# Tap loads ahead of a restacking, 4 KB reads of block inputs, and two kinds of stores on GpSimd's queue, in a hybrid encoder block

## The chip, the cores and the metric

The kernel runs on one core of a Trainium2 chip. A core has a matrix engine (PE), a vector engine (DVE), a scalar engine (ACT), GpSimd (POOL) and SyncE (SP), which here does nothing but issue DMAs. Each engine works off its own instructions in program order; an instruction that waits holds up all that stand behind it on its engine. DMAs are issued by SP, ACT or POOL and carried by 16 DMA engines. The metric is the device time of one execution in microseconds; it is compared as the median of several runs.

## The reference, cut to what matters

One encoder layer for a sequence of 1024 tokens of width 1024, in float32. Every result below is computed; the norms' small helpers are left out.

```
h = RMSNorm_pre(x)
z, xbc, dt_raw, u = split(h @ W_in)            # 1024 | 1536 | 32 | 1024 columns
# SSD mixer (16 heads of 64, 2 groups, state 128, chunks of 128, both directions)
xbc = silu(depthwise_conv5(xbc) + conv_b)
xs, b, c = split(xbc);  dt = softplus(dt_raw + bias);  a = -exp(a_log)
y_f = ssd_scan(xs, dt[fwd], a[fwd], b, c);  y_b = the same on the flipped sequence
y_ssd = group_rms_norm((y_f + y_b + xs * d_skip) * silu(z)) * norm_w
# S5 mixer (64 groups of 16 channels, 64 complex states, both directions)
h_t = A_g h_{t-1} + B_g u_t;   y = Re(C_g h_t) of both directions + d_skip * u
g = gelu(y);   y_s5 = g * sigmoid(g @ glu_w + glu_b)
x = x + RMSNorm_post(concat(y_ssd, y_s5) @ W_out)
# feed-forward
h = RMSNorm_pre(x)
x = x + RMSNorm_post((silu(h @ w_gate) * (h @ w_up)) @ w_down)
```

## The kernel before, in words

A matmul with the precision of float32 is made of three with operands of fewer bits: each operand is split into a high and a low half (`hi`, `lo`), and high by high, low by high and high by low are summed (L276, L1170). All stages below hand tensors to each other over DRAM tiles whose names end in `_d`.

**Stages in order of time.** 0 to 100 us: norm of x, and tables of the S5 powers. 100 to 225: the columns u of the input projection in 8 blocks of 8 groups; `u_evac` (L570 and on) writes a block into `u_d` (8 stores, L580), and `load_u` (L519) reads it back with tokens and channels on partitions. From it come the chunk sums that the S5 recurrence runs over. Up to 420: the other 18 blocks of the projection (`blocks`, L1306: nine of xbc, dt, eight of z, called z0 to z7 here). Between them the S5 recurrence goes on, `pair_down` (L648) finishes it in eight pieces, each four DVE instructions (L651, L652), and *kernel batches* begin. Batch b covers four S5 groups: `xt_load` loads its constants, `c_open` and `c_dir` (L690 to L706) build powers `cp` on ACT and DVE, `k_mm` (L723) multiplies them on PE, and `k_out` (L729 to L731) copies the result to `lg`, adds to it on POOL and stores it into `k_d` from POOL's queue. The number `KC` says how many blocks before the end of the loop over `blocks` batch 0 is opened: at block n the batch n - 18 + KC is opened, and the one before it is multiplied. Four batches are done within the loop.

**The tap stage**, 420 to 520 us, yields the S5 outputs in 16 pieces. `y_mm(i)` (L812 to L814) needs on PE: the taps `W0(i)`, which `w0_load` (L737) loads as a band matrix out of `k_d` from POOL's queue, 424 KB each; the inputs `Uy`, 512 KB for two pieces, loaded by `u_load` (L782) on SP out of `u_d`; `cp`; and the restacked states `AH`, which `restack(i)` (L792 to L802) writes: two POOL memsets for the first two, and eight ACT copies. `restack(0)` stands before the loop's last two blocks, `restack(1)` behind the loop, since it reads the states that the last `pair_down` leaves (and takes its buffer). The stage's loop keeps `w0_load` three pieces ahead, `k_mm` four, `restack` two.

**Up to 690 us** the gated unit of S5 (`glu`) and then `out_s5` run on PE, the second the S5 half of the output projection; its sums go to `m_d`. **SSD units** 0 to 7 (two heads each) are interleaved with these and with `out_g0` by a list scheduler with priorities (the names in `hpri`), so the order on every engine here is the scheduler's. A unit: transposes, `Xw` (L975, one direction on POOL and one on DVE), states `Sn` (PE L988, DVE L999), masked scores `M` (L1034, L1035, one of them on POOL), gating `yg` (L1058, L1059, partly on POOL), `sq`, and the split of the result into the two halves of `hl` (ACT L1073, DVE L1074). The halves are stored into `ch_d` and `cl_d` (L1075, L1076, 512 KB each). `cat` tiles are loaded from there.

**out_g0** (L1186 to L1201), about 840 to 930 us, adds the half of the output projection that the first four units feed, 16 pieces of 128 by 512: load the sum so far, `m` (two buffers, L1195), from `m_d`; load `cat` (L1160); 12 matmuls; add on DVE (L1199); store `m` to `m_d` (L1200). **The last quarter of the projection** follows with the block's first residual (`ld`, `ld2`, `ld3`, `xl`: L1675, L1681, L1686, L1690), and from 1050 us the feed-forward part, which PE fills.

Which queue issues a store is in a table: `Q` maps 's' to SP, 'a' to ACT, 'g' to POOL. 'cq' is the entry of L1075 and L1076, 'mq' the one of L1200.

Of the kernel before, what the change touches and what calls it, by code (L numbers as in the profile page):

```python
# [18 lines left out]
def _ap(t, off, dims):  # L19
# [5 lines left out]
KN = {'s0': -800,  # L25
 'sA': 8,
 'sB': 50,
 'sG': -8,
 'sF': 20,
 'rec': 0,  # L30
 'cb': 8,
 'kb': -100,
 'w0': 0,
# [35 lines left out]
 'gsp': [],  # L69
 'rsd': (1, 4, 7),  # L70
 'hq': 's',
 'cq': 's',
 'mq': 's',
 'pd': ['ef00', 'm00', 'xw1', 'yz0'],
 'yo': 0,
 'up': 0,
# [12 lines left out]
 'us': 'sagagaga',  # L89
 'pc': [],  # L90
 'pk': [0, 1, 3, 4],
 'KC': 7,
 'r1': 6,
 'r3': 0,
 'gs': 'asssssss',
# [36 lines left out]
def hymba_block(ctx, tc, P, out, dbg=None, upto=99):  # L132
# [12 lines left out]
    def pri(n):  # L145
        def deco(f):
            def g(*a, **k):
                with hpri(n):
                    return f(*a, **k)
            return g  # L150
        return deco

    act, dve, pool, pe, sp = nc.scalar, nc.vector, nc.gpsimd, nc.tensor, nc.sync
    aq, gq = nc.scalar, nc.gpsimd
# [18 lines left out]
    def dram(shape, name):  # L173
        return tc.dram_tile(shape, F32, name=name)

    u_d = dram([64, 8, 16, 128], "u_d")
    y12_d = dram([2, 128, 2, 1024 + 16], "y12_d")
    x12_d = dram([2, 128, 1024], "x12_d")
    k_d = dram([32, 64 * 240], "k_d")
# [336 lines left out]
    @pri("lu")  # L516
    def load_u(b):
        U = sa.tile([128, 8, 128], F32, tag="U", name="U")
        sp.dma_start(U, u_d[8 * b:8 * b + 8].rearrange("g s h k -> (s h) g k"))  # L519
        return U  # L520

    def pw4(t, d, n0, nn, g0, ng):
# [45 lines left out]
    def u_half(b, hf):  # L568
        ps = pacc()
        gemm(b, hTh[hf], hTl[hf], HF[0], ps)  # L570
        u_evac(b, hf, ps)

    def u_evac(b, hf, ps):
        if hf == 0:
            ups[b] = io.tile([128, 8, 128], F32, tag="io", name="up")
        up = ups[b]
        act.copy(up[:, ::-1, 64 * hf:64 * hf + 64], ps.rearrange("p (k s) -> p s k", s=8))
        if hf == 1:
            for g in range(8):
                {'a': aq, 's': sp, 'g': gq}[KN['us'][g]].dma_start(u_d[8 * b + g].rearrange("s h k -> h s k"), up[16 * g:16 * g + 16, :, :])  # L580

    def u_block(b):
        ensure(b + 1)
# [51 lines left out]
    def pair_powers():  # L635

        t = rt.tile([128, 2, 2, 32], F32, tag="rm", name="rm")
        a2 = rt.tile([128, 2, 2, 32], F32, name="rcA2")
        b2 = rt.tile([128, 2, 2, 32], F32, name="rcB2")
        dve.tensor_tensor(t, rcB, rcB, op=MUL)  # L640
        dve.tensor_tensor(a2, rcA, rcA, op=MUL)
        dve.tensor_tensor(a2, a2, t, op=SUB)
        dve.scalar_tensor_tensor(b2, rcA, 2.0, rcB, op0=MUL, op1=MUL)
        rcs.extend((a2, b2))
# [16 lines left out]
    def pair_down(d, c):  # L661

        t = ck.tile([128, 63, 2, 8], F32, tag="cacc", name="dn")
        advance(d, 2 - d, 1 + d, 63, 8 * c, 8, t)

    def run_steps(n):
        for _ in range(n):
            j = next(steps, None)
            if j is not None:
                rec_step(j)  # L670
# [6 lines left out]
    def xt_load(b):  # L677
        if b in xts_:
            return
        g0 = 4 * b  # L680
        xt = xts_[b] = ck.tile([128, 2, 4, 16], F32, tag="xtc", name="xtc", bufs=2)
        (gq if b < KN["xtb"] else sp).dma_start(xt.rearrange("p y g h -> p y (g h)"), x12_d.rearrange("y p f -> p y f")[:, :, 16 * g0:16 * g0 + 64])
        yk = yks[b] = ck.tile([128, 2, 80], F32, tag="yk", name="yk", bufs=3)
        (gq if b < KN["xtb"] else sp).dma_start(yk, y12_d[0][:, :, 16 * g0:16 * g0 + 80])
# [7 lines left out]
    def c_open(b):  # L692
        xt = xts_[b]
        pl = (ck, 4) if b % 7 < 4 else (yp, 3)
        cp = cps[b] = pl[0].tile([128, 2, 4, 9, 16], F32, tag="cp", name="cp", bufs=pl[1])
        act.copy(_ap(cp, 0, [[576 + 128, 2], [144, 4], [1, 16]]), xt[:, 0].unsqueeze(1).to_broadcast([128, 2, 4, 16]))

    def c_dir(b, d):
        g0 = 4 * b
        e = pool if 2 * b + d in KN['pcd'] else dve  # L700
        xt, cp = xts_[b], cps[b]
        tm = ck.tile([128, 4, 8, 16], F32, tag="tmc", name="tmc")
        dst = _ap(cp, 16 if d == 0 else 576 + 112, [[144, 4], [16 if d == 0 else -16, 8], [1, 16]])
        e.tensor_tensor(dst, spread(xt[:, 0], 8), pw4(arR, d, 1, 8, g0, 4), op=MUL)
        e.tensor_tensor(tm, spread(xt[:, 1], 8), pw4(aiR, d, 1, 8, g0, 4), op=MUL)
        e.tensor_tensor(dst, dst, tm, op=ADD)  # L706
# [3 lines left out]
    @pri("kb")  # L710
    def k_batch(b):
        k_mm(b)
        k_out(b)
# [19 lines left out]
    @pri("w0")  # L733
    def w0_load(b):

        W0 = W0s[b] = wst.tile([128, 960], F32, tag=("whi", "wlo")[b % 2], name="W0")
        gq.dma_start(W0[:, 0:848], bass.AP(tensor=k_d.tensor, offset=k_d.offset + 960 * b,  # L737
                                           ap=[[16, 8], [64 * 240, 16], [1, 848]]))
# [39 lines left out]
    @pri("u")  # L778
    def u_load(B):
        pl = (yp, 1) if B % 3 == 1 else (wst, 2)  # L780
        U = Us_[B] = pl[0].tile([128, 8, 128], F32, tag="raw", name="Uy", bufs=pl[1])
        sp.dma_start(U, u_d[8 * B:8 * B + 8].rearrange("g s h k -> (s h) g k"))  # L782

    AHs = []

    @pri("rs")
    def restack(b):

        if b < 4:

            AH = (ck if b < 2 else yp).tile([128, 2, 4, 128], F32, name=f"AH{b}", tag=("xpad", "cacc", "AH0", "AH1")[b])
            pool.memset(AH[:, 0, :, 0:1], 0.0)  # L792
            pool.memset(AH[:, 1, :, 127:128], 0.0)
            AHs.append(AH)
        AH, p0 = AHs[b if b < 2 else 2 + b % 2], 2 * b
        for d in range(2):
            for j in range(2):
                for comp in range(2):
                    src = SH[64 * j:64 * j + 64, d, (0 if d == 0 else 1):(127 if d == 0 else 128), comp, p0:p0 + 2]
                    dst = AH[64 * comp:64 * comp + 64, d, :, (1 if d == 0 else 0):(128 if d == 0 else 127)]  # L800
                    dst = dst.rearrange("p (q j) k -> p q j k", j=2)[:, :, j, :].rearrange("p q k -> p k q")
                    (dve.tensor_copy if 1 < b and 4 * d + 2 * j + comp in KN["rsd"] else act.copy)(dst, src)  # L802
# [408 lines left out]
    with tc.manual_schedule(engines={mybir.EngineType.DVE, mybir.EngineType.Activation, mybir.EngineType.PE}):  # L1211
# [28 lines left out]
        gemm_quarter(1, 4)  # L1240
        scale(5)
        u_evac(0, 0, ps0)
        for c in (6, 7):
            norm(c)
# [34 lines left out]
    for b in range(3, 8):  # L1279
        s_batch(b - 3, load_u(b - 3))  # L1280
        if b > 3:
            pair_up(b - 4)
        u_block(b)
    cv = None
    for b in range(5, 8):
        s_batch(b, load_u(b))
        pair_up(b - 1)
        xbc_block(b - 5)
        if cv:
            conv_silu(*cv, one=True)  # L1290
        if b > 5:
            cv = conv_taps(XORD[b - 6], sa)
# [44 lines left out]
    KC = KN["KC"]  # L1337
    downs = [(d, c) for c in range(4) for d in range(2)]
    with tc.manual_schedule():
        next(cvs)  # L1340
        pair_powers()
        for n, blk in enumerate(blocks):
            blk()
            run_steps(KN["r1"])
            next(cvs, None)
            if n == 10:
                run_steps(64)
            if n > 10:
                for _ in range(1 if n < 15 else 2):
                    if downs:  # L1350
                        pair_down(*downs.pop(0))
            b = n - NB + KC
            if 0 <= b < 4:
                c_open(b)
                c_dir(b, 0)
                run_steps(KN["r3"])
                c_dir(b, 1)
            if 0 < b < 5:
                k_batch(b - 1)
            if 0 <= b + 1 < 6:  # L1360
                xt_load(b + 1)
            if n == NB - 3:
                next(cvs, None)
                restack(0)
        restack(1)
        w0_load(0)
        w0_load(1)
        u_load(0)
    rst.close()
    hst[0].close()  # L1370
    hst[1].close()
# [23 lines left out]
    with tc.manual_schedule():  # L1395
        c_open(4)
        c_dir(4, 0)
        c_dir(4, 1)
        w0_load(2)
        u_load(1)  # L1400
        u_load(2)
        qs, oth = [], others()
        for i in range(16):
# [90 lines left out]
    B = {n: hp2.tile([128, 2, 4, 512], F32R, name="B" + n) for n in ("11", "21", "22")}  # L1494
# [85 lines left out]
    bank, us, ts_ = {}, {}, {}  # L1580
# [178 lines left out]
    for l in range(8):  # L1759
        b = MX["step"] * l  # L1760
# [11 lines left out]
        for q in range(2):  # L1772
            at(b + MX["ev"] + 0.6 * q, turn_evac, l, q)
            if l < 4 or q:
                n = "12"[q] + "12"[l // 4]
# [44 lines left out]
    for i in range(14, len(prods)):  # L1820
        p, n, m = prods[i]
# [68 lines left out]
    us, ts_ = C21, C22  # L1890
# [117 lines left out]
```

## Time and profile before

| | |
|---|---|
| median of 3 runs | 1652.74 us (1648.15 to 1654.55) |
| profiled execution | 1652.82 us, span 1651.1 us, mean granted PE clock 0.976 |
| PE | 1532.9 us busy, 93% |
| DVE | 1240.3 us, 75% |
| ACT | 719.5 us, 44% |
| POOL | 372.1 us, 23% |
| DMA | 271.59 MB, mean 164 GB/s |
| chain that ended last | PE 64%, DVE 11%, DMA 11%, ACT 6%, issue 5% |

The span runs from the first to the last instruction on record; the execution's time is 1.72 us longer. POOL's busy time doesn't include the DMAs that it issues. A share for PE over the whole span mixes stages in which it has no gap with stages in which it waits, so the rows below are of single stretches.

### The profile page before, as it was taken

The page shows a single profiled execution, that of the slowest core. Times are in us where ns is not written, and L with a number is a line of the kernel's source. Part 1 is how long each engine was busy: PE and PEld are TensorE (multiplying, and loading weights), DVE is VectorE, ACT ScalarE, POOL GpSimd, SP SyncE. Part 2 cuts the span into 40 slices and gives each one's busy share as a digit, 9 for nine tenths or more (in the row PEclk, how much of TensorE's full clock was granted, in tenths as well). Part 3 has the DMA queues.
Part 4 walks back from the last instruction along what each step waited for, and adds up shares of the span by engine and source line. Part 5 has one row for each costly group of instructions (what it writes and reads, how often), then busy time and mean ns, then how long its engine had stood idle before and what let it go on. Part 6 is the DMA issues. An engine that isn't in the chain of part 4 may idle for free.

```text
span 1651.1 us, 22178 instructions
## 1 busy us (share of the span) xinstructions
PE 1532.9 (93%) x7980; PEld 1256.0 (76%) x7980; DVE 1240.3 (75%) x1997; ACT 719.5 (44%) x1207; POOL 372.1 (23%) x403
## 2 busy tenths in 40 slices
PE   7999999999786989999999787999999999999997
PEld 6777788778675767777778675788888888788886
DVE  6549898877783777876666578788888878669677
ACT  6345532223776454544343387232322333345452
POOL 2100000000221120122210140555555555200001
PEclk9999999999998899999999998999999999999999
DMA  5554444432898557877688883233222221493234
GB/s 182 140 149 108 132 148 153 134 99 93 206 216 206 176 183 255 280 234 228 193 255 259 265 269 105 96 118 111 104 102 96 96 103 58 178 351 108 96 115 179
DMA packets 250001, 271.59 MB, mean 164 GB/s; under 512 B 29387, under 2 KB 190659, under 8 KB 249891
## 3 DMA queue, kind: packets, MB, share of 16 engines
q1 hardware_dynamic: 224515, 215.96, 42.3%
q0 software_dynamic: 12896, 33.83, 6.6%
q10 hardware_dynamic: 12480, 20.39, 3.5%
q8 instruction: 63, 1.03, 0.3%
q14 instruction: 47, 0.39, 0.1%
HBM read 185.23 MB, written 84.84 MB: 164 GB/s over the span
## 4 chain that ended last, share of the span: by engine, by line
PE 64%; DVE 11%; DMA 11%; ACT 6%; issue 5%; POOL 1%; SPq 1%; ACTq 0%; DVEq 0%; POOLq 0%
PE acc L276 17%; PE acc L1589 13%; PE ptmp L1589 10%; PE ptmp L1895 6%; PE acc L1895 5%; PE acc L1170 4%; DMA m<-m_d 2%; DMA m_d<-m 1%; DMA W<-k_d 1%; PE ptmp L557 1%; PE ptmp L1054 1%; PE ptmp L988 1%; DVE cacc L755 1%; PE ptmp L723 1%; DMA cl_d<-ghl 1%
## 5 line engine op out<-in xcount | busy, mean ns | idle before, releaser
L1170 PE MATMUL acc<-ohi,cat 128*128 128x512 f32 x512 | 173.3, 403 | 14.6 <-DVE m L1199 6.9
L276 PE MATMUL acc<-hTh,whi 128*128 128x512 f32 (+1 forms) x456 | 179.4, 394 | 0.4 <-ACT hTh L333 0.4
L276 PE MATMUL acc<-hTl,whi 128*128 128x512 f32 (+1 forms) x456 | 178.3, 391 | 0.5 <-DVE hTl L336 0.5
L276 PE MATMUL acc<-hTh,wlo 128*128 128x512 f32 (+1 forms) x456 | 177.8, 391 | 0.0
L1572 DVE TENSOR_TENSOR wop<-rawp,wop 128x512 fp32r<-128x512 f32 x120 | 137.5, 1147 | 17.9 <-ACT wop L1571 16.7
L1589 PE MATMUL ptmp<-T,wop 128*128 128x512 f32 x528 | 127.6, 398 | 4.1 <-ACT T L1745 3.7
L1589 PE MATMUL acc<-T,wop 128*128 128x512 f32 x528 | 125.7, 393 | 1.9 <-DVE T L1748 1.8
L1170 PEld LDWEIGHTS acc<-ohi,cat 128*128 128x128 f32 x512 | 97.4, 191 | 38.9 <-DVE m L1199 9.4
L1895 PE MATMUL ptmp<-dop 128*128 128x512 f32 x528 | 123.5, 396 | 2.9 <-DVE dop L1877 2.9
L1589 PE MATMUL acc<-B,wop 128*128 128x512 f32 x528 | 124.3, 391 | 0.0
L1589 PEld LDWEIGHTS ptmp<-T,wop 128*128 128x128 f32 x528 | 100.9, 191 | 27.2 <-ACT T L1745 3.9
L1895 PEld LDWEIGHTS ptmp<-dop 128*128 128x128 f32 x528 | 101.1, 192 | 24.6 <-DVE dop L1877 3.2
L1589 PEld LDWEIGHTS acc<-T,wop 128*128 128x128 f32 x528 | 98.8, 188 | 25.2 <-DVE T L1748 3.6
L1589 PEld LDWEIGHTS acc<-B,wop 128*128 128x128 f32 x528 | 99.0, 188 | 21.5
L1604 ACT ACTIVATE cg<-cg 128x512 f32<-128x512 f32 x44 | 27.8, 633 | 182.9 <-DVE cg L1602 182.9
L1571 ACT CAST wop<-rawp 128x512 fp32r<-128x512 f32 x120 | 70.3, 615 | 76.7 <-POOL rawp L1546 51.2
L1170 PE MATMUL acc<-olo,cat 128*128 128x512 f32 x256 | 101.7, 397 | 0.3 <-DVE olo L1134 0.3
L276 PEld LDWEIGHTS acc<-hTh,whi 128*128 128x128 f32 x456 | 86.5, 190 | 19.5 <-issue 1.9
L276 PEld LDWEIGHTS acc<-hTl,whi 128*128 128x128 f32 x456 | 86.6, 190 | 17.9 <-DVE hTl L336 1.0
L276 PEld LDWEIGHTS acc<-hTh,wlo 128*128 128x128 f32 x456 | 86.7, 190 | 17.2 <-DVE wlo L267 0.2
L1876 ACT CAST dop<-da 128x512 fp32r<-128x512 f32 x77 | 48.0, 623 | 99.5 <-PE acc L1895 38.8
L1610 POOL TENSOR_TENSOR cg<-cg 128x512 f32<-128x512 f32 x44 | 61.8, 1404 | 130.8 <-DVE cg L1605 130.2
(367 smaller groups left out, 3340.8 us busy)
## 6 DMA issues: line engine op xcount, KB each, us to landing
ff_d<-cg POOLq DMA_DIRECT2D x77, 256.0 KB, 2.3
da<-ff_d SPq DMA_DIRECT2D x35, 512.0 KB
raw<-in_w_in_dram SPq DMA_DIRECT2D x28, 512.0 KB
cat<-ch_d SPq DMA_DIRECT2D x48, 256.0 KB
cat<-cl_d SPq DMA_DIRECT2D x48, 256.0 KB
wd<-in_w_down_dram SPq DMA_DIRECT2D x44, 256.0 KB
rawp<-in_w_gate_dram SPq DMA_DIRECT2D x10, 1024.0 KB
rawp<-in_w_up_dram SPq DMA_DIRECT2D x10, 1024.0 KB
```

The lines of the kernel that those rows point to most:

```text
L276: pe.matmul(ps, a[:, k, :], b[:, k, sl], start=(k == 0 and n == 0), stop=(k == 7 and n == 2))
L557: pe.matmul(t[64 * j:64 * j + 64, 256 * d + 128 * comp:256 * d + 128 * comp + 128], bm[:, d, g, 64 * comp:64 * comp + 64], U[:, 4 * hb + g ...
L723: pe.matmul(t[32 * g:32 * g + 32, 16 * o:16 * o + 16 * n], st, rhs.rearrange("p n h -> p (n h)"), start=a, stop=z, tile_position=(0, 32 * g))
L755: (pool if ct in KN['pc'] and k in KN['pk'] else dve).scalar_tensor_tensor(a[:, d], xp[:, r], w[k], a[:, d], op0=MUL, op1=ADD)
L1170: pe.matmul(ps, c[:, a, k % 4, :], b[:, k % 2, :], start=(k == 0 and n == 0), stop=(k == n_ - 1 and n == 2))
L1571: act.copy(t[:, 0], src)
L1572: dve.tensor_tensor(t[:, 1], src, t.bitcast(F32)[:, 0], op=SUB)
L1589: pe.matmul(ps, a[:, ai, k, :], b[:, bi, k, :], start=(k == 0 and q == 0), stop=(k == 3 and q == 2))
L1604: act.activation(cg[:, 0], cg[:, 0], AF.Silu)
L1610: pool.tensor_tensor(dst, a, b, op=op)
L1876: act.copy(t[:, k, 0], src)
L1895: pe.matmul(ps, t[:, 0, a, 128 * j:128 * j + 128], t[:, 1, b, :], start=(q == 0 and n == 0), stop=(q == NP - 1 and n == 2))
```

## The change

Four edits. (1) The stores of `hl` ('cq') and of `m` in out_g0 ('mq') go from SP's queue to POOL's. (2) `u_d` is laid out with the groups of a block inside, so that `load_u` and `u_load` read 128 pieces of 4 KB instead of 1024 of 512 bytes; the eight stores of a block still write 512-byte pieces. (3) `KC` is 6 instead of 7: every step of a kernel batch in the loop over blocks comes one block later, and the two blocks with two `pair_down` are now numbers 11 and 16 instead of 15, 16 (and 17, which has none left). (4) `w0_load(0)`, `w0_load(1)` and `u_load(0)` stand ahead of `restack(1)`.

```diff
- 'cq': 's',
- 'mq': 's',
+ 'cq': 'g',
+ 'mq': 'g',
...
- 'KC': 7,
+ 'KC': 6,
...
-    u_d = dram([64, 8, 16, 128], "u_d")
+    u_d = dram([8, 8, 16, 8, 128], "u_d")
...
-        sp.dma_start(U, u_d[8 * b:8 * b + 8].rearrange("g s h k -> (s h) g k"))
+        sp.dma_start(U, u_d[b].rearrange("s h g k -> (s h) g k"))
...
-                {...}[KN['us'][g]].dma_start(u_d[8 * b + g].rearrange("s h k -> h s k"), up[16 * g:16 * g + 16, :, :])
+                {...}[KN['us'][g]].dma_start(u_d[b][:, :, g].rearrange("s h k -> h s k"), up[16 * g:16 * g + 16, :, :])
...
-        sp.dma_start(U, u_d[8 * B:8 * B + 8].rearrange("g s h k -> (s h) g k"))
+        sp.dma_start(U, u_d[B].rearrange("s h g k -> (s h) g k"))
...
-                for _ in range(1 if n < 15 else 2):
+                for _ in range(2 if n in (11, 16) else 1):
...
-        restack(1)
         w0_load(0)
         w0_load(1)
         u_load(0)
+        restack(1)
```

On POOL in front of the tap stage, before: the last kernel batch of the loop (`lg`, `k_d`), the memsets of both `AH`, and the two tap loads (the number in a name is the buffer's).

```order
40 L730 TENSOR_TENSOR lg<-lg,dd 128x16
41 L731 DMA k_d<-lg 4x32x240
42 L792 MEMSET AH_3700 128x4
43 L793 MEMSET AH_3700 128x4
44 L792 MEMSET AH_3833 128x4
45 L793 MEMSET AH_3833 128x4
46 L737 DMA W_3844<-k_d 128x1x848
47 L737 DMA W_3846<-k_d 128x1x848
```

And now.

```order
40 L792 MEMSET AH_3679 128x4
41 L793 MEMSET AH_3679 128x4
42 L730 TENSOR_TENSOR lg<-lg,dd 128x16
43 L731 DMA k_d<-lg 4x32x240
44 L737 DMA W_3833<-k_d 128x1x848
45 L737 DMA W_3835<-k_d 128x1x848
46 L792 MEMSET AH_3839 128x4
47 L793 MEMSET AH_3839 128x4
```

The tap loads have passed the second pair of memsets, and the batch's `lg` and `k_d` have come behind the first pair.

On POOL from SSD unit 7 to the end of out_g0, before: `Xw`, `M` and `yg` of unit 7, and the power of the group norm (L316).

```order
133 L975 TENSOR_TENSOR Xw<-X,wdt 128x1024
134 L1034 TENSOR_TENSOR M<-E 128x512
135 L1058 TENSOR_TENSOR yg<-yg,EF 128x384
136 L1059 TENSOR_TENSOR yg<-yg,zt 128x512
137 L316 TENSOR_TENSOR rg<-rg,mhalf 128x8
```

And now; the numbers at `m` are its 16 buffers in turn, the first `ch_d`, `cl_d` of the rows are unit 6's.

```order
149 L975 TENSOR_TENSOR Xw<-X,wdt 128x1024
150 L1075 DMA ch_d<-hl 128x1024
151 L1076 DMA cl_d<-hl 128x1024
152 L1200 DMA m_d<-m_7635 128x512
153 L1200 DMA m_d<-m_7673 128x512
154 L1034 TENSOR_TENSOR M<-E 128x512
155 L1200 DMA m_d<-m_7693 128x512
156 L1200 DMA m_d<-m_7784 128x512
157 L1058 TENSOR_TENSOR yg<-yg,EF 128x384
158 L1059 TENSOR_TENSOR yg<-yg,zt 128x512
159 L1200 DMA m_d<-m_7846 128x512
160 L1200 DMA m_d<-m_7866 128x512
```

Between `Xw` and `M` of unit 7 there now stand unit 6's two stores and two of `m`, and `Xw` itself comes behind the first four stores of `m`; four more, unit 7's halves and the last four stand behind these rows, ahead of the power.

On SP at the end of out_g0, before: loads and stores of `m`, and between them unit 7's halves.

```order
387 L1200 DMA m_d<-m_7912 128x512
388 L1160 DMA cat<-ch_d 128x4x128
389 L1200 DMA m_d<-m_7970 128x512
390 L1075 DMA ch_d<-hl 128x1024
391 L1076 DMA cl_d<-hl 128x1024
392 L1195 DMA m_7990<-m_d 128x512
393 L1195 DMA m_8021<-m_d 128x512
394 L1160 DMA cat<-cl_d 128x4x128
395 L1663 DMA wpost<-in_norm_mix_post_dram 128x1024
396 L1200 DMA m_d<-m_7990 128x512
397 L1200 DMA m_d<-m_8021 128x512
398 L1686 DMA mix<-m_d 128x1024
```

And now.

```order
360 L1195 DMA m_7912<-m_d 128x512
361 L1195 DMA m_7970<-m_d 128x512
362 L1160 DMA cat<-cl_d 128x4x128
363 L1160 DMA cat<-ch_d 128x4x128
364 L1160 DMA cat<-cl_d 128x4x128
365 L1195 DMA m_7990<-m_d 128x512
366 L1195 DMA m_8021<-m_d 128x512
367 L1195 DMA m_8041<-m_d 128x512
368 L1195 DMA m_8061<-m_d 128x512
369 L1663 DMA wpost<-in_norm_mix_post_dram 128x1024
370 L1686 DMA mix<-m_d 128x1024
371 L1690 DMA xr<-in_x_dram 128x1024 x2
```

The stores are gone from between the loads of `m`, and what follows these loads (`wpost`, `mix`, `xr`) stands right behind them.

## Rows read from the trace of the kernel before

**Rows 1.** the page: busy time of each engine, share of the span

```profile
PE 1532.9 (93%) x7980; PEld 1256.0 (76%) x7980; DVE 1240.3 (75%) x1997; ACT 719.5 (44%) x1207; POOL 372.1 (23%) x403
```

**Rows 2.** stretches: start:end, length, each engine's busy us, granted PE clock, DMA share, GB/s

```profile
425.00:480.00 55.00, 48.17 (x490) 44.71 (x490) 40.32 (x71) 43.33 (x80) 15.48 (x31) 0.93 0.86 215
680.00:840.00 160.00, 151.74 (x872) 124.09 (x872) 117.94 (x223) 76.99 (x103) 29.29 (x18) 1.00 0.72 227
905.00:915.00 10.00, 8.24 (x43) 6.45 (x41) 5.08 (x5) 4.38 (x2) 0.00 (x0) 1.00 0.65 213
915.00:925.00 10.00, 4.51 (x13) 3.63 (x14) 1.79 (x4) 0.79 (x1) 1.66 (x1) 0.66 0.90 289
925.00:938.00 13.00, 11.46 (x49) 8.45 (x47) 5.70 (x8) 2.27 (x5) 0.00 (x0) 1.00 0.87 280
```

**Rows 3.** chain that ended last, before the tap stage: start, us, what

```profile
418.33 6.38 issue
```

**Rows 4.** timeline of POOL: start, us, instruction, idle before it and its releaser

```profile
384.92 0.72 POOL L731 DMA_DIRECT2D k_d<-lg  x1 [0.30 <-POOL lg L730]
...
397.36 0.70 POOL L731 DMA_DIRECT2D k_d<-lg  x1 [0.30 <-POOL lg L730]
...
414.19 0.10 POOL L792 MEMSET AH<- 128x4 f32 x1 [15.97 <-DVE SH L652]
...
414.71 1.22 POOL L737 DMA_DIRECT2D W<-k_d  x2 [0.38 <-issue]
```

**Rows 5.** timeline of ACT at the second restacking

```profile
419.35 5.16 ACT L802 COPY AH<-SH 64x254 f32<-64x254 f32 x8 [0.40 <-DVE tmc L705]
```

**Rows 6.** DMA issues, 412 to 418 and page: KB each, us to landing

```profile
W<-k_d POOLq DMA_DIRECT2D x2, 424.0 KB, 9.8
...
ff_d<-cg POOLq DMA_DIRECT2D x77, 256.0 KB, 2.3
```

**Rows 7.** DMA rate in 40 slices, 412 to 418, then 0 to 9

```profile
GB/s 0 0 0 0 0 0 0 0 0 0 0 0 20 130 256 164 106 137 27 65 113 328 341 348 362 331 386 321 335 338 345 317 321 290 297 287 290 294 466 203
...
GB/s 0 0 0 0 0 0 0 9 171 255 164 221 346 309 400 401 419 419 400 419 400 310 303 332 344 330 341 337 412 371 307 382 382 437 382 419 419 419 400 382
```

**Rows 8.** timeline of DVE, then of PE, at the first kernel block

```profile
346.09 1.21 DVE L651 TENSOR_TENSOR dn<-rcA,SH 128x1008 f32<-128x1008 f32 x1 [7.38 <-DMA xs_d<-cacc]
...
354.80 1.22 DVE L267 TENSOR_TENSOR wlo<-raw,whi 128x1024 fp32r<-128x1024 f32 x1
...
354.98 2.39 PE L723 MATMUL ptmp<-cp,yk 128*32 128x128 f32 x24 [3.27 <-issue]
```

**Rows 9.** chain that ended last, 840 to 940: shares, then pieces in order

```profile
by line: DMA m<-m_d 27.8%; DMA m_d<-m 23.2%; PE acc L1170 7.8%; DVE m L1199 7.0%; DVE hl L1074 4.3%; DMA cat<-ch_d 4.0%; issue 4.0%; ACT hl L1073 3.2%; DVE Sn L999 2.2%; ACT sq L1069 2.1%; PE ptmp L988 2.1%; SPq L1681 1.8%; PE ptmp L1054 1.
...
863.39 0.75 DVE m L1199
...
913.15 2.08 DVE hl L1074
...
916.14 4.84 DMA m<-m_d
```

**Rows 10.** timeline of SP's queue, 905 to 934

```profile
909.27 0.33 SPq L1200 DMA_DIRECT2D m_d<-m  x1
...
915.66 1.21 SPq L1195 DMA_DIRECT2D m<-m_d  x2
...
929.96 0.98 SPq L1200 DMA_DIRECT2D m_d<-m  x2
```

**Rows 11.** timeline of PE, 905 to 940

```profile
920.49 0.80 PE L1170 MATMUL acc<-ohi,cat 128*128 128x512 f32 x1 [5.72 <-DVE m L1199]
...
929.99 0.50 PE L1170 MATMUL acc<-ohi,cat 128*128 128x512 f32 x1 [1.22 <-DVE m L1199]
```

**Rows 12.** timeline of POOL, then its waits: total us, times, longest

```profile
861.02 1.92 POOL L975 TENSOR_TENSOR Xw<-X,wdt 128x1024 f32<-128x1024 f32 x1 [11.59 <-ACT X L904]
...
POOL M L1034 <- ACT E L1015: 111.2, 8, 33.9
```

More of the change, by code (lines that the diff above doesn't have):

```diff
@@ L579, in u_evac @@
             for g in range(8):
-                {'a': aq, 's': sp, 'g': gq}[KN['us'][g]].dma_start(u_d[8 * b + g].rearrange("s h k -> h s k"), up[16 * g:16 * g + 16, :, :])
+                {'a': aq, 's': sp, 'g': gq}[KN['us'][g]].dma_start(u_d[b][:, :, g].rearrange("s h k -> h s k"), up[16 * g:16 * g + 16, :, :])
     def u_block(b):
```

## The prediction, made before the changed kernel was run

> **What bounds the kernel now.** I read the page first, then the busy time by stretches, then the chain of waits in the stretches where PE is not full, then the timelines of the queues there. The page says 93% PE [rows 1], and that is a mean of two kinds of stage. From 680 to 840 us PE works 151.7 of 160 us, so nothing that happens beside it is worth more than the 8.3 us left. In the tap stage it works 48.2 of 55 us, the DMA engines are 86% busy and ACT 43.3 us; at the end of out_g0 it works 4.5 us of the ten from 915 on, at a granted clock of 0.66 [rows 2]. The feed-forward part behind it isn't touched. So the change can earn something at two places: the start of the tap stage, and out_g0.
>
> At the first, PE has finished z7 at 418.33 and does nothing for 6.38 us [rows 3]. The chain calls it "issue", so the releaser has to be found by other rows: the two tap loads leave POOL only at 414.71, because the memset in front of them waits at 414.19, after 15.97 us of idleness, for the states of the last `pair_down`; the preceding store had left at 397.36 [rows 4]. A tap load there takes 9.8 us [rows 6]: 414.71 + 9.8 = 424.5, and the first tap matmul starts at 418.33 + 6.38 = 424.71. The eight copies of the second restacking, from 419.35 for 5.16 us [rows 5], end at the same time but are needed only by piece 1.
>
> At the second, out_g0 has only two buffers for `m`, so load, add, store and the next load run in one ring: 27.8% of the chain from 840 to 940 is loads of `m`, 23.2% stores [rows 9]. SP issues both in program order. At 909.27 it sends a store, then it must wait for unit 7's halves, and the next two loads of `m` leave at 915.66 [rows 10], right after DVE's part of `hl`, which starts at 913.15 and takes 2.08 [rows 9]. PE waits 5.72 us for the additions that need those loads [rows 11].
>
> **The change part by part, against the profiled execution's 1652.8 us** (its span of 1651.1 and 1.7 outside; the median of the runs is 0.1 below, so the same sum serves).
>
> *Tap loads first, batches one block later.* Behind the first pair of memsets POOL now does the last batch's store and then the two tap loads. That store moves one block back: 397.36 plus the 12.4 us that lie between it and its predecessor at 384.92 [rows 4], so 409.8, and the loads leave at about 410.5 instead of 414.71. With 9.8 us they land at about 420. PE's side: the wait for the first kernel batch (PE idle 3.27 us, then 2.39 us of matmuls) doesn't vanish. A `pair_down` is four DVE instructions of 1.21, and the first can start only at 346.09; block 11 now has two of them, so the low weights of z3, at 354.80 before [rows 8], come out at 346.09 + 9.7 + 1.2 = 357.0, when PE went on before as well. But the batch's 2.39 us, then hidden in front of it, now come after a block, with a warm clock some 1.3 us. So z7 ends at 419.7 and the taps are there at 420, 4.7 us before 424.71; the two loads' transfers have fewer others beside them that early, and I take **-5.0**. Piece 1 follows its restacking, which moves from 419.35 to 420.7 and ends at 425.9, while piece 0 and a kernel batch run; it doesn't hold the stage back for longer than before. Bounds: 0, if the 86% busy DMA engines or the copies set the stage's pace whatever its start, to -6.4, the whole gap. The memsets behind the loads cost 0.2 us of POOL, with the restacking still waiting for the states: nothing. `u_load(0)` now comes behind the loads of a batch on SP, and has some 15 us to spare before 420.
>
> *4 KB reads.* The `u_load` reads in pieces of 512 bytes run at 320 to 350 GB/s with little else about, the x tiles in pieces of 4 KB at 400 to 419 [rows 7]: 512 KB in 1.27 instead of 1.55 us, 0.3 us each. The eight of `load_u` lie beside a PE that is full. Of the tap stage's eight, 2.4 us of DMA time, some part shows: **-0.5**, bounds 0 and -2.4. The eight stores of a block keep their 512-byte pieces, at another stride; no row prices that, and they go out beside matmuls of the next block; 0, bounds 0 and +1.
> The Trainium skill ("DMA: Bandwidth & Descriptors", Specifications) puts the smallest transfer at line rate at 512 bytes; by it the reads gain nothing, and the forecast would be 0.5 us higher. The two rates above disagree.
>
> *Stores of `m` and `hl` from POOL.* Four sub-steps at the end of out_g0. (a) The loads that left at 915.66 no longer stand behind unit 7's halves; they need the buffers, the second of whose stores left at 909.27 [rows 10] and lands some 3 us later: loads at about 912, -3.7. (b) PE's gap of 5.72 then shrinks to about 2; the 4.51 us at a granted clock of 0.66, between the two levels of 1.2 and 2.4 GHz [rows 2], would be 3.0 at the full one: I take 1.0 of these 1.5. (c) The last two stores at 929.96 had the last `cat` loads behind them on SP; now these go out before. Of PE's 1.5 idle us from 925 to 938, 1.22 of them before one matmul [rows 11], I take 1.0, and of the 1.8 from 905 to 915 [rows 2], where `cat` loads stand behind stores too, another 1.0: -2.0. (d) Against it: `Xw` of unit 7, which began at 861.02 on POOL [rows 12], stands behind the fourth store of `m`, which can go only after DVE's addition at 863.39 [rows 9]: 864.1 + 0.6 for issuing + 1.9, so it ends at 866.6 instead of 862.9. DVE's half comes behind the same addition, so I take 0.7 of these 3.7. And a store from POOL may be slower than from SP: the chain holds 23.2 us of stores, in five pieces, 4.6 us each; 256 KB from POOL land in 2.3 us in the quiet feed-forward part, a tap load in a busy stretch in 9.8 [rows 6]. I take 0.1 more per store, because the bytes and the busy engines stay the same, +0.5. Sum -3.7 - 1.0 - 2.0 + 0.7 + 0.5 = **-5.5**. Bounds: -8.8 (all of PE's idle time from 905 on, 1.8 + 5.5 + 1.5 [rows 2]) to +17 (rival 3).
> The Trainium skill gives a first byte after about 1 us for GpSimd's path and 0.6 for SP's (same page, Specifications); by it five stores cost 2.0 instead of 0.5, and the forecast would be 1643.3. The rows show no such pair of equal stores.
>
> *Stores of `hl` of units 0 to 6* free SP and put waits on POOL. Behind such a store stands mostly the next unit's `M`, which waited for ACT anyway, 111.2 us in 8 times [rows 12], 14 us each: while one half of `hl` takes DVE 2.08 [rows 9]. PE has at most 8.3 us to give or lose from 680 to 840, and the scheduler swaps a few DVE and ACT rows: **0**, bounds -3 and +3. The group norm's power now comes behind the last store of `m`, some 928, before the last quarter needs it at 935.
>
> Sum: -5.0 - 0.5 - 5.5 = -11.0, so **1641.8 us**.
>
> **The rivals.**
> 1. *Only the tap stage gains.* The DMA engines are 65 to 90% busy around 905 to 938 [rows 2], so freeing SP lets the same bytes queue elsewhere, and the loads of `m` come back no earlier: 1652.8 - 5.5 = 1647.3. For it: 4.84 us for a 256 KB load [rows 9]. Against it: from 909.27 to 915.66 the load wasn't issued at all.
> The Trainium skill says so as a rule (same page, Issuing engines are not separate DMA queues): all queues share 16 engines, and another issuer saves only the issue time. By that rule the landing times stay, and since the blocked 3.7 us are time of SP's own, they would still go: 1643.6 from this rival's 1647.3.
> 2. *Only out_g0 gains.* The tap stage is a chain of ACT copies and transfers on 86% busy engines [rows 2]; starting it 5 us earlier only makes it wait later. 1652.8 - 6.0 = 1646.8. Against it: piece 1's restacking really moves.
> 3. *Slower: a store from POOL lands late.* Every `m` goes once more through the ring of two buffers. If a store takes 8 us, nearer to a tap load's 9.8 than to the 4.6 of now, the five on the chain cost 17, and (a) to (c) are lost with them: 1652.8 + 17 - 5.5 = 1664.3. With (a) to (c) lost it takes back the other gains from 5.7 us per store on (5 x 1.1 = 5.5). For it: 9.8 [rows 6]; against it: 2.3 for the same bytes.
> 4. *The change hardly does what it says:* the restacking or the kernel batch's wait, now a block later, holds piece 0 as long as before, and the stores wait on POOL as they did on SP: 1652.
>
> **How the numbers follow.** Forecast 0.55, rival 1 0.13, rival 2 0.11, rival 3 0.11, rival 4 0.10. A measurement of this kernel tells about 0.5%, 8.3 us, from no change: faster is below 1644.5, slower above 1661. The forecast's own range, 1633 to 1646, is from 2 us more in the tap stage (the whole gap and the reads), 3.5 in out_g0 and 3 between, to 4 less; a tenth of it falls within 0.5%. Faster: 0.55 x 0.9 plus a third of rivals 1 and 2 (units of 680 to 840 may add up to 3) = 0.57; slower 0.11 and a little for a worse scheduler order = 0.12; the rest 0.31. With rivals 1, 2 and 4 inside, the range is 1632 to 1653.
>
> **What would show it.** Right: the first tap matmul at about 420, PE's gap there under 1.5 us; the last loads of `m` from SP at 912, PE's gap of 5.72 under 3, `m_d` stores landing in 4 to 5 us. Wrong: tap loads leaving POOL at 410 but the stage ending at the old time (rival 2); stores of 6 us or more (rival 3); a gap in front of unit 7's state matmuls of several microseconds; PE under 148 us busy from 680 to 840 in a longer stretch.

## The result: 0.6% slower, and the profile after

The changed kernel takes 1663.7 us (median of 11 runs, 1655.3 to 1670.8) against 1652.9 of before in the same rounds (1648.2 to 1658.2). The ratio is 1.006, with a 95% interval of 1.0042 to 1.0079. The forecast was 1641.8 with a range of 1632 to 1653. The profiled execution took 1661.4 us. The page's lines of it, then the five stretches of [rows 2]:

```profile
span 1659.7 us, 22218 instructions
...
PE 1535.8 (93%) x7980; PEld 1259.6 (76%) x7980; DVE 1247.8 (75%) x1997; ACT 720.3 (43%) x1207; POOL 391.5 (24%) x435
```

```profile
425.00:480.00 55.00, 41.45 (x427) 38.63 (x426) 38.49 (x68) 40.82 (x74) 13.62 (x28) 0.91 0.75 193
680.00:840.00 160.00, 152.49 (x875) 124.92 (x874) 118.57 (x219) 76.39 (x103) 35.06 (x28) 1.00 0.72 224
905.00:915.00 10.00, 9.83 (x48) 7.78 (x46) 4.73 (x8) 0.00 (x0) 1.66 (x3) 1.00 0.72 223
915.00:925.00 10.00, 7.55 (x32) 5.90 (x33) 6.90 (x7) 6.48 (x4) 2.72 (x5) 1.00 0.70 253
925.00:938.00 13.00, 8.99 (x40) 7.24 (x38) 2.63 (x3) 0.00 (x0) 1.08 (x2) 0.87 0.85 296
```

PE's total work is about the same. In the tap stage it has become 41.5 of 55 us where it was 48.2, though the stage starts earlier. Around 915 to 925 PE is busy for 7.6 us at full clock where it was 4.5 at 0.66; from 925 on that is taken back, 9.0 of 13 us at a granted clock of 0.87 where it was 11.5 at 1.00. Unit 7 ends some 7 us later than before, so these two windows don't hold quite the same work.

**The tap stage.** PE's timeline; first the first tap matmul, then the first with a long wait.

```profile
418.02 0.46 PE L812 MATMUL ptmp<-Uy,W 128*128 128x128 f32 x2
...
436.33 1.09 PE L903 MATMUL ptmp<-ident,BT 128*128 128x128 f32 x4 [8.85 <-DMA BT<-xs_d]
```

The stage starts at 418.0 without a gap, so the 6.38 us of [rows 3] are gone, as forecast and 2 us earlier than the 420 that I gave it. But 18 us later PE waits 8.85 us for `BT`, the SSD input B, which comes next on PE: `ssd_prep` transposes it (L903) behind pieces 0 and 1. Its load on SP; then, of the kernel before, SP's row for this load and PE's for the transposes:

```profile
418.03 1.32 SPq L833 DMA_DIRECT2D dvec<-in_ssd_d_dram  x2
...
424.18 0.33 SPq L908 DMA_DIRECT2D BT<-xs_d  x1
```

```profile
429.74 0.33 SPq L908 DMA_DIRECT2D BT<-xs_d  x1
...
435.15 1.09 PE L903 MATMUL ptmp<-ident,BT 128*128 128x128 f32 x8
```

The load is issued 5.6 us earlier than before and lands no earlier: the transposes begin at 436.33, where they began at 435.15 without a wait. A gap of 6.38 us in front of piece 0 has become one of 8.85 behind piece 1. In front of the load on SP's queue are two loads of `dvec`, the 16 numbers `ssd_d`, which L833 reads as 1024 pieces of 4 bytes. The DMA view of 424 to 430 of the kernel after (rate in 40 slices, packets, SP's queue `q1`, and the one load of POOL issued there):

```profile
GB/s 248 281 202 237 320 275 401 273 328 383 328 220 138 56 82 28 28 28 28 1 0 0 0 1 0 0 0 0 0 0 0 0 0 0 0 2 5 1 34 28
DMA packets 856, 0.59 MB, mean 99 GB/s; under 512 B 723, under 2 KB 723, under 8 KB 856
...
q1 hardware_dynamic: 700, 0.01, 6.2%
...
W<-k_d POOLq DMA_DIRECT2D x1, 424.0 KB, 15.3
```

For the last 3 us the rate is next to nothing, with over 1.5 MB issued: in these 6 us SP's queue moves 700 packets that hold 0.01 MB together. On POOL's queue a tap load takes 15.3 us in this time.

**The end of out_g0.** POOL's timeline; the four rows of 845 and later are the fourth store of `m` and `Xw` of unit 7, the low half of unit 7, and the two stores of `m` behind it.

```profile
409.59 1.22 POOL L737 DMA_DIRECT2D W<-k_d  x2
...
868.33 0.54 POOL L1200 DMA_DIRECT2D m_d<-m  x1 [5.20 <-DVE m L1199]
868.89 1.92 POOL L975 TENSOR_TENSOR Xw<-X,wdt 128x1024 f32<-128x1024 f32 x1
...
922.34 0.55 POOL L1076 DMA_DIRECT2D cl_d<-hl  x1 [1.78 <-DVE hl L1074]
923.00 1.21 POOL L1200 DMA_DIRECT2D m_d<-m  x2
```

The tap loads went out at 409.6, as forecast. `Xw` began at 868.89, right behind the store, 7.9 us later than in [rows 12]. On DVE, the addition that this store waited for, DVE's half of `Xw` with the row in front of it, and unit 7's `hl`; then these two rows of before:

```profile
867.29 0.75 DVE L1199 SCALAR_TENSOR_TENSOR m<-acc,rg,m 128x512 f32<-128x512 f32 x1 [4.33 <-DMA m<-m_d]
...
868.67 2.70 DVE L1058 TENSOR_TENSOR yg<-yg,EF 128x512 f32<-128x512 f32 x1
871.29 1.21 DVE L975 TENSOR_TENSOR Xw<-X,wdt 128x1024 f32<-128x1024 f32 x1
...
919.81 2.23 DVE L1074 SCALAR_TENSOR_TENSOR hl<-yg,vec,hl 128x1024 fp32r<-128x1024 f32 x1 [1.09 <-ACT hl L1073]
```

```profile
864.06 0.68 DVE L1058 TENSOR_TENSOR yg<-yg,EF 128x512 f32<-128x512 f32 x1
864.66 1.22 DVE L975 TENSOR_TENSOR Xw<-X,wdt 128x1024 f32<-128x1024 f32 x1
```

The addition was 3.9 us later than in [rows 9], and unit 7's `hl` came at 919.8 instead of 913.15. DVE's half of `Xw` came 6.6 us later: it stands behind the same addition, and behind a `yg` that took 2.70 us beside POOL's late `Xw`, for 0.68 before, where the two don't overlap. PE's timeline after, and behind it PE's row of before for the state matmuls:

```profile
872.56 4.87 PE L988 MATMUL ptmp<-Xw,Bt 128*128 128x128 f32 x28 [6.61 <-DVE Xw L975]
...
922.75 0.50 PE L1170 MATMUL acc<-ohi,cat 128*128 128x512 f32 x1 [1.03 <-DVE m L1199]
...
930.73 0.80 PE L1170 MATMUL acc<-olo,cat 128*128 128x512 f32 x1 [4.01 <-DVE olo L1134]
```

```profile
866.02 4.94 PE L988 MATMUL ptmp<-Xw,Bt 128*128 128x128 f32 x28 [3.41 <-DVE Xw L975]
```

PE's wait of 5.72 us for an addition [rows 11] has shrunk to 1.03, and in its place are 6.61 instead of 3.41 for `Xw` (DVE's half, which comes last) and 4.01 for an operand. SP's loads of `m`, a row of four:

```profile
918.54 8.61 SPq L1195 DMA_DIRECT2D m<-m_d  x4
```

They take 8.6 us of SP's time, because the buffers of the last two come free only with stores that POOL sends at 923.0, behind unit 7's halves. The waiting place that the change took from SP stands on POOL now.

### The profile page after: what moved, and what is told of

Read it like the earlier page. It is cut to its first block, busy times and chain, and to the rows that moved or that the text cites. A ratio compares the mean times of both kernels' runs of the same rounds, so it can differ in the third digit from the quotient of the medians.

```text
span 1659.7 us, 22218 instructions
## 1 busy us (share of the span) xinstructions
PE 1535.8 (93%) x7980; PEld 1259.6 (76%) x7980; DVE 1247.8 (75%) x1997; ACT 720.3 (43%) x1207; POOL 391.5 (24%) x435
## 3 DMA queue, kind: packets, MB, share of 16 engines
q8 instruction: 63, 1.03, 0.3%
## 4 chain that ended last, share of the span: by engine, by line
PE 63%; DMA 12%; DVE 9%; issue 7%; ACT 6%; POOL 2%; SPq 1%; POOLq 0%; DVEq 0%; ACTq 0%
PE acc L276 18%; PE acc L1589 13%; PE ptmp L1589 10%; PE ptmp L1895 6%; PE acc L1895 5%; PE acc L1170 4%; PE ptmp L557 2%; DMA m_d<-m 1%; DMA BT<-xs_d 1%; DMA m<-m_d 1%; DMA raw<-in_s_glu_w_dram 1%; DMA cat<-ch_d 1%; PE ptmp L1054 1%; DVE dop L1877 1%; DMA g_d<-G 1%
## 6 DMA issues: line engine op xcount, KB each, us to landing
ff_d<-cg POOLq DMA_DIRECT2D x77, 256.0 KB, 2.3
cat<-ch_d SPq DMA_DIRECT2D x48, 256.0 KB
cat<-cl_d SPq DMA_DIRECT2D x48, 256.0 KB
wd<-in_w_down_dram SPq DMA_DIRECT2D x44, 256.0 KB
```

## The experiments

Four times are read from each kernel's profiled execution: the start of z7's last matmul, of the gated unit's last, of DVE's part of unit 7's `hl`, and of the output projection's last matmul. The table has the stretches between them in us; ratios are to before in the same five rounds (seven to twelve runs of a kernel). The stretches are of one execution each. Those of `a_both_sp`, `b_tap` and `a_m_sp` are of one 7.6, 5.8 and 3.6 us above the kernel's median, that of `b_stores` of one 4.0 below; the others lie within 2.3 us of theirs.

| kernel | ratio (95%) | z7 to gated unit | to `hl` of unit 7 | to projection's end |
|---|---|---|---|---|
| before | | 250.0 | 245.4 | 68.1 |
| after | 1.0060 (1.0042 to 1.0079) | 249.0 | 253.4 | 67.0 |
| b_stores | 1.0044 (1.0027 to 1.0061) | 248.3 | 253.3 | 67.8 |
| a_both_sp | 1.0034 (1.0014 to 1.0053) | 261.0 | 245.0 | 68.1 |
| a_m4 | 1.0051 (1.0030 to 1.0072) | 254.5 | 249.1 | 68.6 |
| a_m_sp | 1.0047 (1.0027 to 1.0068) | 253.3 | 244.2 | 71.6 |
| b_tap | 0.9995 (0.9974 to 1.0017) | 256.0 | 244.6 | 67.4 |
| b_dvec | 0.9997 (0.9977 to 1.0018) | 250.8 | 245.8 | 68.6 |
| a_dvec | 1.0026 (1.0008 to 1.0044) | 242.0 | 254.8 | 66.4 |
| a_both_sp_dvec | 0.9961 (0.9943 to 0.9979) | 244.6 | 244.1 | 67.4 |
| d_hl_sp | 1.0036 (1.0013 to 1.0059) | 244.3 | 256.5 | 69.1 |
| d_free | 0.9993 (0.9970 to 1.0017) | 241.3 | 250.5 | 68.0 |
| d_m3 | 1.0003 (0.9978 to 1.0028) | 247.2 | 239.9 | 82.1 |
| d_hl7_act | 0.9971 (0.9949 to 0.9993) | 241.2 | 246.0 | 68.3 |
| e_tap_dvec | 0.9940 (0.9913 to 0.9967) | 241.3 | 244.1 | 69.1 |
| e_hl_pool | 0.9968 (0.9950 to 0.9986) | 239.3 | 245.8 | 71.3 |

**First: which edits lose.** `a_both_sp` has `'cq': 's', 'mq': 's'` in the kernel after; `b_stores` has `'cq': 'g', 'mq': 'g'` in the kernel before.

> The changed kernel with both kinds of stores back on SP, so only the layout of u_d, the later kernel batches and the earlier tap loads are left of the change. Theory (GpSimd's in-order queue ties the additions of out_g0 to SSD unit 7): the loss is gone, 1650 to 1654 us; Xw of unit 7 on GpSimd starts within 2 us of its input again, the first tap matmul stays at 418, and the tap stage still ends within 2 us of before. Rival (layout or later batches cost): 1660 or more.

> The kernel before with only the two kinds of stores moved to GpSimd. Theory: the whole loss, 1660 to 1666 us, Xw of unit 7 some 6 to 8 us late. Rival (the loss comes from the other three edits): 1651 to 1655.

Both are slower, so the loss has two parts and my theory had one. `b_stores` fits it, with 8 us more up to unit 7's `hl`, though its 1658.6 us are 1.4 below its range. `a_both_sp` doesn't (1658.8 us): that stretch is as before, but the one in front of it has 11 us more in this execution, the slowest of its twelve. PE's timeline of `a_both_sp` has the wait of after again:

```profile
438.42 1.94 PE L903 MATMUL ptmp<-ident,BT 128*128 128x128 f32 x8 [9.73 <-DMA BT<-xs_d]
```

The next two split the stores: the first four of `m` on SP, and all of `m` on SP.

```diff
-                Q[KN["mq"]].dma_start(m_d[l][:, HF[cb_]], m)
+                (sp if 8 * cb_ + l < 4 else Q[KN["mq"]]).dma_start(m_d[l][:, HF[cb_]], m)   # a_m4
...
- 'mq': 'g',
+ 'mq': 's',                                                                                  # a_m_sp
```

> The changed kernel with the first four of the 16 stores of m back on SP, the other twelve and all halves of hl on GpSimd. Theory: Xw of unit 7 no longer stands behind an addition, starts right after its input (861 to 864), unit 7 ends 5 us earlier, 1654 to 1659 us; what is left is the stores 13 and 14 behind unit 7's halves. Rival (a store from GpSimd is slower wherever it stands): 12 of 16 stores are as slow as now, 1661 or more.

> The changed kernel with all stores of m back on SP, halves of hl on GpSimd. Theory: neither Xw behind an addition nor additions behind halves, SP no longer waits for unit 7's halves: 1647 to 1653 us. Rival (the halves hold up each unit's instructions behind them on GpSimd): 1658 or more.

The times missed (1662.2 and 1659.9 us), since PE waited for B in both, 8.69 and 9.30 us. The stretch up to `hl` says more: 249.1 and 244.2, where it is 253.4 with all stores on POOL. In `a_m4`, `Xw` waits for its input and not for a store:

```profile
872.21 1.91 POOL L975 TENSOR_TENSOR Xw<-X,wdt 128x1024 f32<-128x1024 f32 x1 [14.66 <-ACT X L904]
```

That is 197.8 us behind the gated unit's end, against 202.5 after and 193.3 before: half of the delay is gone. The input itself is late now.

**Second: the pieces of 4 bytes.** `dvec` is loaded whole, and sorted on the chip:

```diff
-        for j in range(2):
-            sp.dma_start(dvec[64 * j:64 * j + 64, :],
-                         P["ssd_d"].rearrange("(q j) -> j q", j=2)[j].partition_broadcast(64))
+        d16 = sper.tile([128, 16], F32, name="d16")
+        sp.dma_start(d16, P["ssd_d"].partition_broadcast(128))
+        for j in range(2):
+            act.copy(dvec[64 * j:64 * j + 64, :], d16[64 * j:64 * j + 64].rearrange("p (q j) -> p j q", j=2)[:, j])
```

It is put into `a_both_sp`, into before (`b_dvec`) and into after (`a_dvec`); `b_tap` is before with edit 4 alone.

> The changed kernel with all stores back on SP, and ssd_d loaded as 128 contiguous pieces of 64 bytes and sorted by two small ACT copies, in place of 1024 pieces of 4 bytes. Theory (in the tap stage B's load stands behind those 1024 pieces on SP's DMA queue, and PE's in-order queue behind B's transposes): PE's wait of 9.7 us for B falls under 2, the transposes start before 430 instead of at 438, the tap stage ends 8 to 12 us earlier than with the stores alone moved back (525), 1643 to 1650 us. Rival (the earlier tap loads and the 4 KB reads fill the engines, and B lands late through them): the transposes still start at 436 or later, 1657 to 1660.

> The kernel before with the contiguous load of ssd_d alone. Theory: there B landed just in time, so little changes: 1647 to 1652 us, the first tap matmul still at 422 to 425 after a gap of 6 to 7 us. Rival (the small pieces hold up the whole stage in either kernel): 1640 to 1646.

> The kernel before with the two tap loads and the first block of inputs ahead of the second restacking, batches and layout as before. Theory: piece 0 starts 4 to 6 us earlier and PE then waits 6 to 10 us for B, the stage ends within 3 us of before: 1650 to 1657. Rival (the layout or the later batches are what costs): 1644 to 1648, B on time.

> The changed kernel, whole, with the contiguous load of ssd_d. Theory: the loss of the tap stage goes, that of out_g0 stays (about 7 us): 1650 to 1656, and 6 to 9 below the changed kernel. Rival: 1660 or more.

The theory held in the main point of all four: medians of 1646.7, 1654.2, 1651.2 and 1655.9 us. `b_dvec` lies 2 us over its range, with no change against before in its own rounds (0.9997). `a_both_sp` to `a_both_sp_dvec`: 1.0034 to 0.9961, 12 us of the whole, and 261.0 to 244.6 us in this stretch, where 8 to 12 were expected. SP's issues and PE's row of `a_both_sp_dvec`:

```profile
419.54 0.34 SPq L833 DMA_DIRECT2D d<-in_ssd_d_dram  x1
...
423.17 0.33 SPq L909 DMA_DIRECT2D BT<-xs_d  x1
```

```profile
430.43 1.06 PE L904 MATMUL ptmp<-ident,BT 128*128 128x128 f32 x8 [1.18 <-ACT AH L802]
```

PE waits 1.18 us in place of 9.73, and for ACT; the transposes start at 430.4, just missing the 430 that I gave them. The DMA view of the same 424 to 430:

```profile
GB/s 269 248 229 193 284 208 248 217 302 230 359 362 396 387 389 350 352 247 288 245 302 229 250 168 277 170 248 303 219 329 410 437 410 437 418 399 376 429 318 434
DMA packets 952, 1.85 MB, mean 309 GB/s; under 512 B 553, under 2 KB 553, under 8 KB 952
...
W<-k_d POOLq DMA_DIRECT2D x1, 424.0 KB, 7.0
```

The mean of these 6 us is 309 instead of 99 GB/s (1.85 MB for 0.59), and POOL's tap load lands in 7.0 us for 15.3. The same view gives 109 and 142 GB/s for `a_both_sp` and `b_tap`, with the tap load at 15.7 and 15.0 us, and 318 and 281 for `a_dvec` and `e_tap_dvec`, with 7.8 and 6.4. In `b_tap`, which has neither the later batches nor the new layout, PE waits for B as in after:

```profile
436.18 1.94 PE L903 MATMUL ptmp<-ident,BT 128*128 128x128 f32 x8 [8.43 <-DMA BT<-xs_d]
```

And `b_dvec` shows why nothing of it could be seen before: with the tap stage starting at 424.7 in before and 424.6 here, B's transposes start without a wait in both, and mending the load alone changes nothing. By whole times edit 4 alone, with the small pieces, is worth nothing (`b_tap`, 0.9995), and `a_both_sp`, which adds edits 2 and 3 to it, is 0.4% slower than that (1.0034; the intervals just overlap). So with the pieces in place the later batches or the new layout may cost something as well. These two weren't run apart.

**Third: how the stores lose**, with `dvec` mended in all. `d_hl_sp` is `a_dvec` with `'cq': 's'`. `d_free` is `a_dvec` with the edit of `a_m4` and unit 7's halves on ACT. `d_m3` and `d_hl7_act` start from `a_both_sp_dvec`: three buffers of `m` for two (`bufs=3` at `mt` and `m0`), and unit 7's halves on ACT (`hq_ = aq if q == 7 else Q[KN["cq"]]`).

> The changed kernel with the contiguous load of ssd_d and the halves of hl back on SP, all stores of m on GpSimd. With all stores on SP this kernel needs 311 us from the gated unit's last matmul to the output projection's last, with all on GpSimd 321. Theory (Xw of unit 7 behind the fourth store of m costs about half of that, the halves in front of the stores 13 and 14 most of the rest): 315 to 317 in that stretch, 1649 to 1653 us. Rival (any store of m from GpSimd costs): 319 or more, 1654 or more.

> The changed kernel with the contiguous load of ssd_d, the first four stores of m on SP and unit 7's halves on ACT; the other twelve stores of m and fourteen halves stay on GpSimd. Theory (two places in GpSimd's order make the whole loss, not the queue itself): Xw of unit 7 starts right after its input, the stretch from the gated unit's last matmul to the output projection's last takes 309 to 313 us, 1643 to 1648 us. Rival (stores from GpSimd's queue are slower): 317 or more, 1651 or more.

> All stores on SP, contiguous load of ssd_d, and three buffers for m instead of two. Theory of the prediction (the ring of load, add, store sets the end of out_g0): the stretch falls from 311 to 305 to 308 us, 1640 to 1644 us. Rival (unit 7 sets the end, the ring only fills the time beside it): 310 to 312, 1645 to 1648 us.

> All stores on SP but unit 7's two halves, which go from ACT, and the contiguous load of ssd_d. It tries step (a) of the prediction alone: SP no longer waits for these halves in front of the loads of m. If the step holds: PE's wait of 5 us before the last additions goes, the stretch falls from 311 to about 308, 1642 to 1645 us. Rival (unit 7 itself ends the stretch): 310 to 312, 1645 to 1648 us.

My theory of two places missed twice. With the stores of `m` alone on POOL, `d_hl_sp` loses as much as with both (1.0036, `a_dvec` 1.0026, the intervals overlap): 325.6 us from the gated unit to the projection's end and 1657.5 us in all, as its rival had it. `Xw` again stands right behind a store:

```profile
865.62 1.92 POOL L976 TENSOR_TENSOR Xw<-X,wdt 128x1024 f32<-128x1024 f32 x1
```

`d_free` is 4.3 us better than `a_dvec` up to `hl` and 0.33% in time (the intervals overlap a little), but not the 10 that I gave it: clearing POOL's order in front of `Xw` brings about half. Its time of 1650.3 us lies between theory and rival; its 318.5 us to the projection's end are the rival's. One tie that is left is on DVE, where the last gating of unit 7 stands behind an addition that waits for its load of `m`. DVE's timeline of `d_free`:

```profile
903.80 0.75 DVE L1201 SCALAR_TENSOR_TENSOR m<-acc,rg,m 128x512 f32<-128x512 f32 x1 [4.60 <-DMA m<-m_d]
904.47 0.55 DVE L1059 TENSOR_TENSOR yg<-yg,EF 128x384 f32<-128x384 f32 x1
905.05 0.69 DVE L1060 TENSOR_TENSOR yg<-yg,zt 128x512 f32<-128x512 f32 x1
```

But that order is not new: the last gating stands behind such an addition in the kernel before too, which waits 4.08 us for its load, and in `a_both_sp_dvec`, which waits 3.09. It can explain 1.5 of the 6.4 us that `d_free` has more than `a_both_sp_dvec` up to `hl`. Of the rest, some lies in front of `Xw`, which starts right after its input and still 4.4 us later than there, counted from the gated unit's end. But a late `Xw` isn't passed on in full: in `e_hl_pool` below it is 3.3 us later and `hl` 1.7. So the cause of this other half stays open.

`d_m3` widens the ring by a third buffer, and unit 7 is 4 us earlier than in any other kernel; the projection's end comes 82 us behind it, and its time of 1655.6 us is over both ranges. PE now waits for `cat`; why that is late was not looked into:

```profile
909.98 0.47 PE L1171 MATMUL acc<-ohi,cat 128*128 128x512 f32 x1 [2.88 <-DMA cat<-ch_d]
...
927.92 1.22 PE L1171 MATMUL acc<-ohi,cat 128*128 128x512 f32 x2 [8.43 <-DMA cat<-cl_d]
```

`d_hl7_act` is step (a) of the prediction by itself. PE's wait for an addition, 4.71 us in `a_both_sp_dvec`, is gone in it; 2.24 for an operand and 2.31 for `cat` stand in its place. It gains nothing over `a_both_sp_dvec` (0.9971 and 0.9961).

**Fourth: what carries the gain.** `e_tap_dvec` is before with edit 4 and the mended load; `e_hl_pool` is `a_dvec` with `'mq': 's'`.

> The kernel before with the earlier tap loads and the contiguous load of ssd_d; batches and layout as before, stores on SP. Theory (the tap loads give the gain once B is not behind the small pieces): from z7's last matmul to the gated unit's last 243 to 246 us, against 250 before and 256 with the tap loads alone, 1645 to 1649 us. Rival (the later batches or the 4 KB reads are needed for the gain): 248 or more, 1650 to 1653 us.

> The changed kernel with the contiguous load of ssd_d and the stores of m back on SP, so the halves of hl alone on GpSimd. Theory (the halves cost little; the additions' stores in GpSimd's order cost most of the 10 us that a_dvec loses against all stores on SP): 2 to 4 us more than with all stores on SP, 1648 to 1651 us. Rival (the halves cost as much as the stores of m): 1652 or more.

Both held; the first is 1.5 us below its range (1643.5), the second (1649.0) loses 1.2 us by the ratios against all stores on SP, which is within the noise. `e_tap_dvec` is the fastest of all, 0.994 of before: the later batches and the 4 KB reads aren't needed for it. The halves on POOL cost 0 to 2 us up to `hl` (`a_m_sp`, `e_hl_pool`) and 3.5 to 3.9 from there to the projection's end; the stores of `m` cost the rest.

## Why the prediction was wrong

The ratio makes +9.9 us where -11.0 were forecast. By the experiments the stores account for 12.8 of these 20.9 us (+7.3 for -5.5) and the tap loads for 5.0 (0 for -5.0, with the small pieces in place). The rest isn't assigned to an edit.

**Tap loads, -5.0.** The start came 6.7 us earlier, more than forecast. The first step that failed is the sentence that piece 1's restacking "doesn't hold the stage back for longer than before", and the bound of 0 to -6.4: I followed PE only to piece 1 and didn't ask what is next on it. The next is B's transposes, and B was late by what SP had issued in front of it. I took the -5.0 for the stage's; with the small pieces in the way edit 4 brought nothing (`b_tap`, 0.9995), and without them -9.9 (`e_tap_dvec`, 0.9940). The stretch from z7 to the gated unit says the same for the second: 241.3 us in `e_tap_dvec`, 250.0 before. With the pieces it scatters from 249.0 (after) to 261.0 (`a_both_sp`), and its highest values are of executions well above their kernel's median. Rival 2 named the outcome, a stage that waits later, but by busy engines; for 3 us of PE's wait they were nearly idle.

**Later batches.** z7's last matmul starts at 419.2 in the mean of the eleven kernels with `KC` 6, at 416.7 in the five with 7: +2.5 for the +1.3 that I gave it. Each group scatters by 3 to 4 us, the pair of this document shows no delay (417.6 after, 417.9 before), and the new layout is in the same eleven, so its part isn't separate.

**4 KB reads, -0.5.** Nothing of it shows: `a_both_sp_dvec`, with the new layout and the later batches, has 0.9961, `e_tap_dvec` without them 0.9940, and the intervals overlap. The two edits weren't run apart. The Trainium skill ("DMA: Bandwidth & Descriptors", Specifications), by which pieces of 512 bytes are at line rate already, fits that better than my rates, though no run here prices it alone.

**Stores, -5.5.** This is the second step that failed, and the larger: they cost 7.3 us (`b_stores`, 1.0044). Steps (a) and (b) happened, though not at the 912 of the forecast: the loads that left 2.5 us behind unit 7's `hl` left at 918.54, 1.3 us ahead of it; PE's wait fell from 5.72 to 1.03, and the clock stayed up until 925. They were worth nothing. By the table the premise failed that the ring of `m` sets the end of out_g0: from unit 7's `hl` to the projection's end it takes 66.4 to 69.1 us in 13 of the 16 kernels, with ends from 971 to 993 us; the other three are `d_m3` and the two with the halves alone on POOL. That unit 7 ends this part is read from the table, and not shown by an experiment of its own. And `d_hl7_act` did (a) alone and gained nothing. The mis-sized term is then (d): I took 0.7 us for `Xw` behind the store, with the addition at its time of before. But the addition is itself late in the ring, and `Xw` was 9 us late against the gated unit's end (193.3 to 202.5), `hl` 8. Of the 3.7 that I worked out as its bound I took a fifth, on the ground that DVE's half waits as well. It does, and it is the half that PE waits for; but it came later too, by the addition and by the slowed `yg`, which also took 2.70 us in `b_stores`, `a_dvec` and `d_hl_sp`.

**Rival 3** forecast a slower kernel by late landings of POOL's stores, 5.7 us and more. The stores on the chain of after, start and duration:

```profile
885.11 5.97 DMA m_d<-m
...
896.10 6.06 DMA m_d<-m
...
907.24 3.94 DMA m_d<-m
...
923.65 3.12 DMA m_d<-m
```

They take 4.8 us in the mean of four, for 4.6 before. So the landing hardly changed, which fits the rule of the Trainium skill (same page, Issuing engines are not separate DMA queues) that the DMAs of all issuers run on the same 16 engines. The other half of that rule, that another issuer only saves issue time, came out the other way here. The loss is in what stands behind a store on its engine.

## What to carry to other kernels

A start that is made earlier is worth what the next instruction on that engine allows: follow the engine's order on until the first operand that can't come earlier, with the queue that brings it. A store moved to an engine that also computes turns every wait of that store into a wait of what stands behind it there; look for the late chain among those, before the ring that the store belongs to. A load in pieces of a few bytes belongs where nothing that is waited for follows it soon on its queue.

## What the runs showed of the hardware

Two loads of 2 KB, in 1024 pieces of 4 bytes together, held SP's queue for over 10 us (issued at 418.0 to 419.4, B's load behind them landed at about 436 in after). The 16 engines moved 99 to 142 GB/s from 424 to 430 in three kernels with these pieces and 281 to 318 in three without; in after they were nearly idle for 3 us of it. A 424 KB load on POOL's queue took 15.0 to 15.7 us with them and 6.4 to 7.8 without. I hadn't expected that from 4 KB of data.

A DVE instruction `yg` of 128 by 512 took 2.70 us in the four kernels in which POOL's `Xw` began beside it, and 0.68 in before, where it didn't.
